# Two-bank score tiles, joint masked halves, and an eleventh weight pair in a hybrid attention and retention block

## The chip, the core and the metric

The kernel runs on one core of one Trainium2 chip. The metric is the device time of one execution in microseconds (us). A core has five engines that run at once, each through its own instruction stream: TensorE (PE in the profile; PEld is its weight load), VectorE (DVE), ScalarE (ACT), GpSimd (POOL) and SyncE (SP), which here only issues transfers. SBUF is the on-chip memory; PSUM is the memory that TensorE writes to, in eight banks, each a row of 512 float32 per partition.

## The reference

One decoder block on a sequence of 1024 with a model width of 1024. A single projection of the normalised input gives all branches; retention (A) and windowed attention (B) are gated, summed and projected, and a SwiGLU layer follows.

```python
h = rms_norm(x, ln1_g[l])
proj = h @ w_in[l] + b_in[l]
rq, rk, rv, rg, aq, ak, av, gate_a, gate_b = jnp.split(proj, SPLIT_IDX, axis=-1)
...
ay = sliding_window_sink_attention(aq, ak, av.reshape(B, S, ATTN_KV_HEADS, ATTN_HEAD_DIM), attn_sinks[l])
branch_b = ay.reshape(B, S, ATTN_Q) @ w_attn_out[l]
merged = jax.nn.sigmoid(gate_a) * branch_a + jax.nn.sigmoid(gate_b) * branch_b
x = x + merged @ w_out[l]
```

In the attention 16 query heads share 2 key/value heads. Queries stand in blocks of 128; each block sees its own and the previous block of keys, cut to a window of 128, and a sink value per head enters maximum and denominator:

```python
m = jnp.maximum(jnp.max(scores, axis=-1, keepdims=True), sink)
e = jnp.exp(scores - m)
probs = e / (jnp.sum(e, axis=-1, keepdims=True) + jnp.exp(sink - m))
out = jnp.einsum('bnhgqk,bnkhd->bnqhgd', probs.astype(v.dtype), vb)
```

## The kernel before, in words

Every product of matrices is made of float32 operands split in two, a high and a low part, and takes three matmuls of 128x512 (high x high, high x low, low x high). The split costs ScalarE a cast (the high part) and VectorE a subtraction (the low part) for each weight tile.

The program runs in stages: normalisation and the key and value projections of the attention, then the attention itself with part of the other projections as fill, then the v projection of the retention, the "w" stage, the retention core, the output projections and the SwiGLU layer.

**The attention.** A unit is one query block `b` (0 to 7) of one quad `g` (0 to 3) of four heads: 32 units. `u_scores` makes eight matmuls of 256 columns into two PSUM tiles "s" of a bank each (for `b = 0` the columns are half as many). Since a position of the window lies in exactly one of the two key blocks, ScalarE copies one block's scores to the tile `sc`, and VectorE overwrites the masked places with the other's (L537). A reduction takes the minimum with the sink, ScalarE takes four exponentials (L547, one per head, with their sums), VectorE the reciprocal, and the product normalises `sc`. Two iterations later `u_transpose` turns `sc` by TensorE and splits it into `ph` and `pl`; VectorE also makes masked halves `qh` and `ql` of them (L573), and `u_values` makes four matmuls: `ph`, `pl` with the values of one block, `qh`, `ql` with the difference of two blocks' values.

The result holds, for each head, two halves of sums that have still to be added. For quads 0 and 1, ScalarE copies it to `xy` and GpSimd issues a store to `xy_d`. For quads 2 and 3 the halves are added and split at once (L593 to L599), in place of the queries, and SP stores four parts of 1 MB to `ay_d`. In those quads half of the normalisation is done by ScalarE (L556).

The loop at L646 has 34 iterations. Iteration i takes unit i-2 through `u_transpose`, unit i through `u_scores`, then some steps of fill, then unit i-2 through `u_values`. A fill step is three matmuls 128x512 of the next item in the list `items`: the query projections of quads 1 to 3 (`QuadQ`: four times 24 matmuls, with a turning by ten operations of VectorE and four of ScalarE on each half) and twelve gate tiles (`Gate`: 2 x 24 matmuls). The steps are spread evenly, 244 in 34 iterations, and `fl.until` makes sure that a quad's queries are there before its units. TensorE and SP keep the program order in this loop. On VectorE and ScalarE a scheduler chooses the order, but for the splits of weights and of probabilities, which `tie` holds in program order. All engines then run their streams strictly in order.

**The v projection and the w stage.** The v projection is 28 products of a Strassen-Winograd scheme. VectorE first adds up its operands (`vadd`, L738) in `vacc`, which lies where the attention's buffers were. The w stage multiplies ten pairs of weight tiles (`cols`), each pair by seven products P1 to P7 of twelve matmuls instead of eight: pairs 0 to 7 are the retention's keys, queries and gates, the last two are four gate tiles. GpSimd makes the differences of weights (`gsub`, L676). `wseq` is the order of the products; splits are prepared three products ahead (`wprep_to`). P1, P6, P7 and P4 sum in one bank, and ScalarE copies it between them (`keep`, L968). At the end of this stage `split_ay` adds and splits the stored halves of quads 0 and 1 in eight pieces, one per product.

Of the kernel before, what the change touches and what calls it, by code (L numbers as in the profile page):

```python
# [35 lines left out]
def f32(t):  # L36
    return t.bitcast(F32)
# [3 lines left out]
def hybrid_block(ctx: ExitStack, tc: tile.TileContext, x, ln1_g, w_in, b_in, ret_norm_g, w_ret_out,  # L41
# [21 lines left out]
    ay_d = dram.tile([4, P, 4, S], F32, name="ay_d")  # L63
    xy_d = dram.tile([2, P, 4, S], F32, name="xy_d")
# [5 lines left out]

    def ps(tag, bufs, name):
        return psum.tile([P, 512], F32, tag=tag, bufs=bufs, name=name)

    def acc(name):
        return ps("acc", 3, name)

# [237 lines left out]
    with tc.tile_pool(name="gt", bufs=1, side="right") as gt, tc.tile_pool(name="w1", bufs=1) as w1:  # L314
# [7 lines left out]
        vodd = w1.tile([P, NB // 2, P], F32, tag="pl", bufs=1, name="vodd")  # L322
# [10 lines left out]
        lv = lo.rearrange("p k (z v e) -> p k z v e", z=2, v=2, e=32)  # L333
        def ak_evac(half, pt):
            c = slice(half * 512, half * 512 + 512)
            xb = r512(("ph", "qh")[half], 1, f"kxb{half}")
# [18 lines left out]
        def av_evac(half, pt):  # L355
            vt = r512("ql", 1, f"vt{half}")
# [159 lines left out]
        def u_scores(u):  # L516
# [9 lines left out]
            for jp in range(2):  # L526
                pt = ps("s", 2, f"s{g}{b}{jp}")
                for jj in range(2):
                    j = 2 * jp + jj
                    o = pt[:, jj * 256:jj * 256 + nk]  # L530
                    nc.tensor.matmul(o, Bt[:, jb + j, qc], kst[:, kv, 0, k0:k0 + nk], start=True, stop=False)
                    nc.tensor.matmul(o, Bt[:, jb + j, qc], kst[:, kv, 1, k0:k0 + nk], start=False, stop=True)
                jr = slice(2 * jp, 2 * jp + 2)
                if b > 0:
                    ptv = pt.rearrange("p (j z s) -> p j z s", j=2, z=2)
                    nc.scalar.copy(sc[:, jr, 0:P], ptv[:, :, 1])
                    nc.vector.copy_predicated(sc[:, jr, 0:P], mk.bitcast(U32).rearrange("p (o s) -> p o s", o=1)  # L537
                                              .to_broadcast([P, 2, P]), ptv[:, :, 0])
                    nc.vector.tensor_reduce(out=nm[:, jr], in_=sc[:, jr, 0:P + 1], op=ALU.min,  # L539
                                            axis=mybir.AxisListType.X)  # L540
                for jj in range(2):
                    j = 2 * jp + jj
                    if b == 0:
                        nc.vector.tensor_tensor_reduce(out=sc[:, j, 0:P], in0=pt[:, jj * 256:jj * 256 + P], in1=mk,
                                                       scale=1.0, scalar=nsink[:, 4 * g + j:4 * g + j + 1],
                                                       op0=ALU.add, op1=ALU.min, accum_out=nm[:, j:j + 1])
                    nc.scalar.activation(sc[:, j, 0:P + 1], sc[:, j, 0:P + 1], AF.Exp, scale=-1.0,  # L547
                                         bias=nm[:, j:j + 1], accum_out=den[:, j:j + 1])
            rd = tiny.tile([P, 4], F32, tag="rd", name=f"rd{g}{b}")
            nc.vector.reciprocal(rd, den)  # L550
            nd = 4 if g < 2 else 2
            nc.vector.tensor_tensor(out=sc[:, 0:nd, 0:P], in0=sc[:, 0:nd, 0:P],
                                    in1=rd[:, 0:nd].rearrange("p (j o) -> p j o", o=1).to_broadcast([P, nd, P]),
                                    op=ALU.mult)
            for j in range(nd, 4):
                nc.scalar.activation(sc[:, j, 0:P], sc[:, j, 0:P], AF.Copy, scale=rd[:, j:j + 1])  # L556

        def u_transpose(u):
            g, b, nk, Bt, jb, qc = geo(u)
            sc = scs.pop(u)  # L560
            pt = ps("t", 2, f"pT{g}{b}")
            for j in range(4):
                nc.tensor.transpose(pt[:, j * P:(j + 1) * P], sc[:, j, 0:P], ident)
            ph, pl = (w1.tile([P, 512], F32R, tag=t, bufs=1, name=f"{t}{g}{b}") for t in ("ph", "pl"))
            tie(acts, nc.scalar.copy(ph, pt))
            tie(vecs, nc.vector.tensor_tensor(out=pl, in0=pt, in1=f32(ph), op=ALU.subtract))
            phs[u] = [(vev[:, b // 2], ph, pl)]
            if b > 0:
                mk = amask[:, P:2 * P].rearrange("p (o s) -> p o s", o=1).to_broadcast([P, 4, P])
                part = []  # L570
                for t, src in (("qh", ph), ("ql", pl)):
                    o = w1.tile([P, 512], F32R, tag=t, bufs=1, name=f"{t}{g}{b}")
                    nc.vector.scalar_tensor_tensor(out=o.rearrange("p (j q) -> p j q", j=4), in0=mk,  # L573
                                                   scalar=float(b % 2 - 1), op0=ALU.add,
                                                   in1=f32(src).rearrange("p (j q) -> p j q", j=4), op1=ALU.mult)
                    part.append(o)
                phs[u].append((vdf[:, b - 1], *part))

        def u_values(u):
            g, b, nk, Bt, jb, qc = geo(u)  # L580
            pv = ps("pv", 1, f"pv{g}{b}")
            parts = phs.pop(u)
            for n, (vb, *hl) in enumerate(parts):
                for z, p in enumerate(hl):
                    nc.tensor.matmul(pv, vb[:, g // 2, :], p, start=(n + z == 0), stop=(n == len(parts) - 1 and z == 1))
            t = w1.tile([P, 512], F32, tag="xy", bufs=2, name=f"xy{g}{b}")
            if g < 2:
                nc.scalar.copy(t, pv)
                nc.gpsimd.dma_start(xy_d[g, :, :, qc], t.rearrange("p (j q) -> p j q", j=4))
                return  # L590
            pvv = pv.rearrange("p (i z q) -> p i z q", i=2, z=2)
            tm = t[:, 0:2 * P].rearrange("p (i q) -> p i q", i=2)
            nc.scalar.copy(tm[0:64], pvv[64:128, :, 0, :])  # L593
            nc.scalar.copy(tm[64:128], pvv[0:64, :, 1, :])
            nc.vector.tensor_tensor(out=tm[0:64], in0=pvv[0:64, :, 0, :], in1=tm[0:64], op=ALU.add)
            nc.vector.tensor_tensor(out=tm[64:128], in0=pvv[64:128, :, 1, :], in1=tm[64:128], op=ALU.add)
# [13 lines left out]
        order = list(range(6, 16)) + [0, 1]  # L610
        items = [QuadQ(0), QuadQ(1), Gate(order[0]), QuadQ(2), Gate(order[1]), QuadQ(3)] + [Gate(n) for n in order[2:]]
# [29 lines left out]
        run(filling(0))  # L641
        fl = Fill([filling(n) for n in range(1, len(items))])
        NU = 4 * NB
        fl.step(20)
        left = 32 * 8 - 8 - 4
        with in_order(nc.tensor.engine, nc.sync.engine):  # L646
            for i in range(NU + 2):
                if i % NB == 0 and 0 < i < NU:
                    fl.until((1, 3, 5)[i // NB - 1])
# [1395 lines left out]
```

## Time and profile before

| | |
|---|---|
| median of three runs | 1553.43 us (1551.37 to 1553.9) |
| profiled execution | 1554.05 us |
| its span in the trace | 1551.2 us |
| granted TensorE clock | 0.999 of full speed |
| attention with its fill | about 60 to 336 us of the span |
| v projection, then w stage | 336 to 413, 413 to 605 us |

The span runs from the first to the last instruction in the trace; the time of an execution has some 3 us more around it. A line of a timeline gives start, duration, engine, line of the kernel, operation, output and inputs; in brackets stands the idle time of the engine before it and what ended that. Matmuls overlap, so the distance of two starts, and not the duration shown, is what one costs. In the groups by shape a row ends with the busy time, the mean of one in ns, and the idle time before.

### The profile page before, as it was taken

How to read it: one execution, taken by the hardware profiler on the slowest of the kernel's cores; microseconds unless marked ns; L12 is line 12 of the kernel's file. 1: busy time of each engine (PE TensorE's matmuls, PEld its weight loads, DVE VectorE, ACT ScalarE, POOL GpSimd, SP SyncE). 2: the span in 40 equal slices, each digit the busy share in tenths (PEclk: the TensorE clock that was granted, in tenths of full speed). 3: DMA queues.
4: the chain of work that ended last, by engine and by line, in shares of the span. 5: the costliest groups of instructions: out<-in, count | busy, mean ns of one | idle time of the engine just before them, and what ended most of it. 6: DMA issues, size and time to landing. Idle time of an engine off the chain costs nothing.

```text
span 1551.2 us, 20530 instructions
## 1 busy us (share of the span) xinstructions
PE 1538.7 (99%) x7323; PEld 1284.9 (83%) x7323; DVE 1028.3 (66%) x1674; ACT 705.0 (45%) x1436; POOL 386.7 (25%) x336
## 2 busy tenths in 40 slices
PE   9999999999999999999999999999999999999998
PEld 8888888878888888888888888888888888888886
DVE  7578877788467675887457788444444444678656
ACT  6366677733233344544223465333333333444445
POOL 2001100000235440100111125655555555100001
PEclk9999999999999999999999999999999999999999
DMA  6665464331574456654556203333333333863233
GB/s 228 193 203 178 139 192 171 113 115 55 165 206 140 136 163 232 210 194 137 188 178 237 103 1 109 121 104 102 102 103 102 102 102 102 309 240 95 90 108 122
DMA packets 156402, 228.47 MB, mean 147 GB/s; under 512 B 10027, under 2 KB 82541, under 8 KB 156045
## 3 DMA queue, kind: packets, MB, share of 16 engines
q1 hardware_dynamic: 154972, 222.85, 44.3%
q0 software_dynamic: 1280, 4.20, 0.8%
q8 instruction: 57, 0.93, 0.2%
q14 instruction: 45, 0.36, 0.1%
q10 hardware_dynamic: 48, 0.13, 0.0%
HBM read 152.42 MB, written 69.99 MB: 143 GB/s over the span
## 4 chain that ended last, share of the span: by engine, by line
PE 86%; DVE 5%; ACT 4%; DMA 3%; issue 1%; SPq 0%; POOL 0%; POOLq 0%; DVEq 0%; ACTq 0%
PE fA L1669 15%; PE fB L1669 8%; PE dA L1971 7%; PE wA L963 6%; PE dxP L1971 6%; PE fC L1669 4%; PE wB L963 3%; PE va L807 3%; PE wo L1503 3%; PE woP L1503 2%; PE vP L807 2%; PE acc_ba L167 2%; PE acc_ba L169 2%; PE acc_ba L168 2%; PE acc_bb L167 2%; PE acc_bb L168 2%
## 5 line engine op out<-in xcount | busy, mean ns | idle before, releaser
L1971 PE MATMUL dA<-dwP,daP 128*128 128x512 f32 x528 | 120.6, 389 | 0.0
L1971 PEld LDWEIGHTS dA<-dwP,daP 128*128 128x128 f32 x528 | 99.1, 188 | 20.7 <-DVE dwP L143 0.2
L1971 PE MATMUL dxP<-dwP,daP 128*128 128x512 f32 x396 | 90.2, 389 | 0.0
L1971 PEld LDWEIGHTS dxP<-dwP,daP 128*128 128x128 f32 x396 | 74.3, 188 | 15.4
L167 PE MATMUL acc_g<-h,wh_g 128*128 128x512 f32 x192 | 75.3, 392 | 0.0
L168 PE MATMUL acc_g<-h,wh_g 128*128 128x512 f32 x192 | 74.9, 390 | 0.0
L169 PE MATMUL acc_g<-h,wl_g 128*128 128x512 f32 x192 | 74.8, 389 | 0.0
L547 ACT ACTIVATE sc<-sc,nm 128x129 f32<-128x129 f32 x128 | 50.2, 395 | 43.7 <-DVE nm L539 32.7
L1744 POOL TENSOR_TENSOR xf<-xf 128x512 f32<-128x512 f32 x40 | 62.3, 1557 | 30.3 <-issue 28.9
L523 POOL COPY sc<-nsink 128x4 f32<-128x4 f32 x32 | 9.9, 308 | 238.7 <-issue 73.0
L1675 POOL TENSOR_TENSOR xf<-xf 128x512 f32<-128x512 f32 x33 | 47.3, 1434 | 59.0 <-ACT xf L1677 26.9
L1876 POOL TENSOR_TENSOR rs_f<-tot,mhalf 128x1 f32<-128x1 f32 x8 | 4.8, 606 | 205.4 <-DVE tot L1873 205.4
L143 DVE TENSOR_TENSOR dwP<-wd,dwP 128x512 fp32r<-128x512 f32 x77 | 53.0, 688 | 4.3 <-ACT dwP L140 4.3
L140 ACT CAST dwP<-wd 128x512 fp32r<-128x512 f32 x77 | 47.4, 616 | 8.7 <-PE dA L1971 6.3
L140 ACT CAST daP<-daP 128x512 fp32r<-128x512 f32 x42 | 26.0, 621 | 55.4 <-PE dxP L1971 26.7
L167 PE MATMUL acc_bb<-ay,wh_bb 128*128 128x512 f32 x128 | 51.1, 400 | 0.0
L168 PE MATMUL acc_bb<-ay,wh_bb 128*128 128x512 f32 x128 | 50.1, 391 | 0.0
L169 PE MATMUL acc_bb<-ay,wl_bb 128*128 128x512 f32 x128 | 50.1, 391 | 0.0
L676 POOL TENSOR_TENSOR wr_wp<-wr_wp 128x512 f32<-128x512 f32 x10 | 15.7, 1570 | 137.9 <-DVE w0P L143 119.1
L167 PE MATMUL aq<-h,wh_aq 128*128 128x512 f32 x128 | 50.1, 391 | 0.0
L168 PE MATMUL aq<-h,wh_aq 128*128 128x512 f32 x128 | 50.0, 391 | 0.0
L167 PE MATMUL acc_ba<-yg,wh_ba 128*128 128x512 f32 x128 | 49.9, 390 | 0.0
(847 smaller groups left out, 4351.8 us busy)
## 6 DMA issues: line engine op xcount, KB each, us to landing
act_d<-xf SPq DMA_DIRECT2D x77, 256.0 KB, 2.1
daP<-act_d SPq DMA_DIRECT2D x21, 512.0 KB, 3.6
q<-q_d SPq DMA_DIRECT2D x32, 256.0 KB, 4.0
wr_daP<-act_d SPq DMA_DIRECT2D x14, 512.0 KB, 3.6
wr_g<-in_w_in SPq DMA_DIRECT2D x12, 512.0 KB, 5.9
tb_d<-tb SPq DMA_DIRECT2D x24, 256.0 KB, 4.9
wd<-in_w_ffn_down SPq DMA_DIRECT2D x6, 1024.0 KB, 13.5
wr_f<-in_w_ffn_gate SPq DMA_DIRECT2D x11, 512.0 KB, 4.0
```

Source lines behind the costliest of these rows:

```text
L140: nc.scalar.copy(hi, raw)
L143: return nc.vector.tensor_tensor(out=lo, in0=raw, in1=f32(hi), op=ALU.subtract)
L167: nc.tensor.matmul(pt, hi[:, k, :], xh, start=(k == 0), stop=False)
L168: nc.tensor.matmul(pt, hi[:, k, :], xl, start=False, stop=False)
L169: nc.tensor.matmul(pt, lo[:, k, :], xh, start=False, stop=(k == 7))
L547: nc.scalar.activation(sc[:, j, 0:P + 1], sc[:, j, 0:P + 1], AF.Exp, scale=-1.0, bias=nm[:, j:j + 1], accum_out=den[:, j:j + 1])
L807: nc.tensor.matmul(vbanks[pr][tt], x_[:, c], w[:, u, :], start=(fresh and k + z == 0), stop=(k == 3 and z == 2), skip_group_check=not fresh)
L963: nc.tensor.matmul(pt, o[:, w, k, :], v, start=(first and k + z == 0), stop=(k == 3 and z == 2), skip_group_check=not first)
L1503: nc.tensor.matmul(bank, v[:, q + u, k, c], w[y][:, k % 2, :], start=(first and z == 0), stop=(last and z == 2), skip_group_check=not tracked)
L1669: nc.tensor.matmul(pt, o[:, w, k, :], v, start=(first and n == 0), stop=(n == 11), skip_group_check=not first)
L1744: nc.gpsimd.tensor_tensor(out=o, in0=a, in1=b, op=op)
L1971: nc.tensor.matmul(banks[tt], a[:, u, c], w[:, v, :], start=(fresh and f + z == 0), stop=(f == NP - 1 and z == 2), skip_group_check=not fresh)
```

## The change

Four things change together.

1. The scores of a unit go into one PSUM tile of two banks, with one copy, one predicated copy and one reduction for all four heads. `ph` and `pl` become one tile `p`, and one operation of 128x1024 makes both masked halves `q`.
2. All quads are treated alike: ScalarE copies to `xy`, GpSimd stores to `xy_d` (32 stores instead of 16, of 256 KB), VectorE normalises all four heads. The sums and splits of quads 2 and 3 leave the attention; they become eight more pieces in the w stage, each with two loads, a sum, a cast, a low part and a store of 512 KB to `ay_d` by SP. The first eight pieces go to other products (from P6 of pair 8).
3. Gate tiles 0 and 1 leave the fill and become an eleventh pair. The last pair's order is P6, P5, P7, P2, P4, P3; before it was P6, P7, P5, P4, P3 with P2 made earlier.
4. The fill has ten gate tiles: seven steps an iteration for the first 16, then 96 steps over 18; 28 steps follow the loop, 24 before.

```diff
-            for jp in range(2):
-                pt = ps("s", 2, f"s{g}{b}{jp}")
...
-                    nc.scalar.copy(sc[:, jr, 0:P], ptv[:, :, 1])
-                    nc.vector.copy_predicated(sc[:, jr, 0:P], mk.bitcast(U32).rearrange("p (o s) -> p o s", o=1)
-                                              .to_broadcast([P, 2, P]), ptv[:, :, 0])
...
+            pt = spool[1].tile([P, 4, 2 * P], F32, tag="s4", name=f"s{g}{b}")
...
+                nc.scalar.copy(sc[:, :, 0:P], pt[:, :, P:2 * P])
+                nc.vector.copy_predicated(sc[:, :, 0:P], mk.bitcast(U32).rearrange("p (o s) -> p o s", o=1)
+                                          .to_broadcast([P, 4, P]), pt[:, :, 0:P])
+                nc.vector.tensor_reduce(out=nm, in_=sc[:, :, 0:P + 1], op=ALU.min, axis=mybir.AxisListType.X)
...
+                q = w1.tile([P, 2, 512], F32R, tag="q", bufs=1, name=f"q{g}{b}")
+                nc.vector.scalar_tensor_tensor(out=q.rearrange("p z (j q) -> p (z j) q", j=4), in0=mk,
+                                               scalar=float(b % 2 - 1), op0=ALU.add,
+                                               in1=f32(p).rearrange("p z (j q) -> p (z j) q", j=4), op1=ALU.mult)
...
-            if g < 2:
-                nc.scalar.copy(t, pv)
-                nc.gpsimd.dma_start(xy_d[g, :, :, qc], t.rearrange("p (j q) -> p j q", j=4))
-                return
...
-            v = Bt[:, jb:jb + 4, qc].rearrange("p (i z) q -> p i z q", z=2)
-            nc.scalar.copy(v[:, :, 0, :], tm)
-            nc.vector.tensor_tensor(out=v[:, :, 1, :], in0=tm, in1=f32(v[:, :, 0, :]), op=ALU.subtract)
+            nc.scalar.copy(t, pv)
+            nc.gpsimd.dma_start(xy_d[g, :, :, qc], t.rearrange("p (j q) -> p j q", j=4))
...
-        order = list(range(6, 16)) + [0, 1]
+        order = list(range(6, 16))
...
-        left = 32 * 8 - 8 - 4
+        early, late = 16 * 7, 96
...
-    cols += [C_GA + 256, C_GA + 512]
+    cols += [C_GA + 256, C_GA + 512, C_GA]
...
-        wseq += [(j, "P6"), (j, "P5"), (j, "P7"), (j + 1, "P1")] if nx else [(j, "P6"), (j, "P7"), (j, "P5")]
-        wseq += [(j, "P4"), (j, "P3")] + ([(j + 1, "P2")] if nx else [])
+        wseq += [(j, "P6"), (j, "P5"), (j, "P7"), (j + 1, "P1") if nx else (j, "P2"), (j, "P4"), (j, "P3")]
+        wseq += [(j + 1, "P2")] if j + 2 < NW else []
...
+    at8 = wseq.index((8, "P6"))
+    ayat = [(at8 + n, n) for n in range(8)] + list(zip((23, 26, 30, 37, 40, 44, 51, 54), range(8, 16)))
```

The scheduler's order on VectorE and ScalarE changes with it. Iteration 5 of the loop on VectorE before: `sc_1291` are the scores of unit 5, `ph_1283`, `pl_1284`, `qh_1287` and `ql_1289` the parts of unit 3, whose values end the same iteration.

```order
L566 TENSOR_TENSOR pl_1284<-pT_1278,ph_1283 128x512
L573 SCALAR_TENSOR_TENSOR qh_1287<-amask,ph_1283 128x512
L573 SCALAR_TENSOR_TENSOR ql_1289<-amask,pl_1284 128x512
L537 COPY_PREDICATED sc_1291<-amask,s_1295 128x2x128
L537 COPY_PREDICATED sc_1291<-amask,s_1305 128x2x128
L539 TENSOR_REDUCE nm_1293<-sc_1291 128x2 x2
L483 TENSOR_TENSOR st_1399<-q_1321,atab 128x512
L486 TENSOR_TENSOR q_1321<-q_1321,atab 128x512
L550 RECIPROCAL rd_1315<-den_1294 128x4
L552 TENSOR_TENSOR sc_1291<-sc_1291,rd_1315 128x4x128
```

The same iteration on VectorE after the change: `sc_1195` and `sc_1264` are units 4 and 5, `p_1259` and `q_1262` unit 3.

```order
L558 RECIPROCAL rd_1215<-den_1198 128x4
L559 TENSOR_TENSOR sc_1195<-sc_1195,rd_1215 128x4x128
L547 COPY_PREDICATED sc_1264<-amask,s_1268 128x4x128
L549 TENSOR_REDUCE nm_1266<-sc_1264 128x4
L558 RECIPROCAL rd_1284<-den_1267 128x4
L559 TENSOR_TENSOR sc_1264<-sc_1264,rd_1284 128x4x128
L452 TENSOR_TENSOR wl_aq_1235<-wr_aq_1053,wh_aq_1234 128x512
L570 TENSOR_TENSOR p_1259<-pT_1254,p_1259 128x512
L575 SCALAR_TENSOR_TENSOR q_1262<-amask,p_1259 128x1024
```

Unit 3's parts moved from ahead of unit 5's scores to behind all of that unit's operations. On ScalarE, before, in the same iteration:

```order
L588 COPY xy_1275<-pv_1270 128x512
L565 CAST ph_1283<-pT_1278 128x512
L536 COPY sc_1291<-s_1295 128x2x128
L536 COPY sc_1291<-s_1305 128x2x128
L474 ACTIVATE q_1321<-aq_1248,bcol 128x512
L547 ACTIVATE sc_1291,den_1294<-sc_1291,nm_1293 128x129 x4
```

And after:

```order
L589 COPY xy_1251<-pv_1246 128x512
L555 ACTIVATE sc_1195,den_1198<-sc_1195,nm_1197 128x129 x4
L546 COPY sc_1264<-s_1268 128x4x128
L555 ACTIVATE sc_1264,den_1267<-sc_1264,nm_1266 128x129 x4
L451 CAST wh_aq_1234<-wr_aq_1053 128x512
L569 CAST p_1259<-pT_1254 128x512
```

The cast of unit 3's probabilities moved behind the exponentials of units 4 and 5. In iteration 14 the same stands once more, with unit 14's scores ahead of unit 12's parts, but without an older unit's exponentials.

The end of the w stage on TensorE, before (`w9P` are the splits of the last pair's products, `wA` the bank that P1, P6, P7 and P4 share):

```order
L963 MATMUL wA_5566<-s_3677,w9P_5611 128x512 x12
L963 MATMUL wA_5566<-s_3677,w9P_5634 128x512 x12
L963 MATMUL wB_5696<-h_115,w9P_5656 128x512 x12
L963 MATMUL wA_5566<-h_116,w9P_5673 128x512 x12
L963 MATMUL wB_5696<-s4h,w9P_5693 128x512 x12
```

And after, where `w10P` is the eleventh pair:

```order
L957 MATMUL wA_5366<-s_3258,w10P_5381 128x512 x12
L957 MATMUL wB_5439<-h_118,w10P_5399 128x512 x12
L957 MATMUL wA_5366<-s_3258,w10P_5418 128x512 x12
L957 MATMUL wC_5479<-h_119,w10P_5435 128x512 x12
L957 MATMUL wA_5366<-h_119,w10P_5452 128x512 x12
L957 MATMUL wB_5439<-s4h,w10P_5476 128x512 x12
```

P6 and P7 (the first two in `wA`) now have P5 between them, and P2 (`wC`) stands between P7 and P4.

More of the change, by code (lines that the diff above doesn't have):

```diff
@@ new lines, in u_scores @@
+            pt = spool[1].tile([P, 4, 2 * P], F32, tag="s4", name=f"s{g}{b}")
+            for j in range(4):
+                for z in range(2):
+                    nc.tensor.matmul(pt[:, j, 0:nk], Bt[:, jb + j, qc], kst[:, kv, z, k0:k0 + nk], start=(z == 0),
+                                     stop=(z == 1))
+            if b > 0:
+                nc.scalar.copy(sc[:, :, 0:P], pt[:, :, P:2 * P])
+                nc.vector.copy_predicated(sc[:, :, 0:P], mk.bitcast(U32).rearrange("p (o s) -> p o s", o=1)
+                                          .to_broadcast([P, 4, P]), pt[:, :, 0:P])
+                nc.vector.tensor_reduce(out=nm, in_=sc[:, :, 0:P + 1], op=ALU.min, axis=mybir.AxisListType.X)
@@ new lines, in u_scores @@
+            for j in range(4):
+                if b == 0:
+                    nc.vector.tensor_tensor_reduce(out=sc[:, j, 0:P], in0=pt[:, j, 0:P], in1=mk, scale=1.0,
+                                                   scalar=nsink[:, 4 * g + j:4 * g + j + 1], op0=ALU.add, op1=ALU.min,
+                                                   accum_out=nm[:, j:j + 1])
+                nc.scalar.activation(sc[:, j, 0:P + 1], sc[:, j, 0:P + 1], AF.Exp, scale=-1.0, bias=nm[:, j:j + 1],
+                                     accum_out=den[:, j:j + 1])
@@ L549, in u_scores @@
             rd = tiny.tile([P, 4], F32, tag="rd", name=f"rd{g}{b}")
             nc.vector.reciprocal(rd, den)
[L551 to L556, printed above, removed]
+            nc.vector.tensor_tensor(out=sc[:, :, 0:P], in0=sc[:, :, 0:P],
+                                    in1=rd.rearrange("p (j o) -> p j o", o=1).to_broadcast([P, 4, P]), op=ALU.mult)
@@ L563, in u_transpose @@
                 nc.tensor.transpose(pt[:, j * P:(j + 1) * P], sc[:, j, 0:P], ident)
[L564 to L567, printed above, removed]
+            p = w1.tile([P, 2, 512], F32R, tag="p", bufs=1, name=f"p{g}{b}")
+            tie(acts, nc.scalar.copy(p[:, 0], pt))
+            tie(vecs, nc.vector.tensor_tensor(out=p[:, 1], in0=pt, in1=f32(p[:, 0]), op=ALU.subtract))
+            phs[u] = [(vev[:, b // 2], p)]
             if b > 0:
[L569 to L577, printed above, removed]
+                mk = amask[:, P:2 * P].rearrange("p (o s) -> p o s", o=1).to_broadcast([P, 8, P])
+                q = w1.tile([P, 2, 512], F32R, tag="q", bufs=1, name=f"q{g}{b}")
+                nc.vector.scalar_tensor_tensor(out=q.rearrange("p z (j q) -> p (z j) q", j=4), in0=mk,
+                                               scalar=float(b % 2 - 1), op0=ALU.add,
+                                               in1=f32(p).rearrange("p z (j q) -> p (z j) q", j=4), op1=ALU.mult)
+                phs[u].append((vdf[:, b - 1], q))
         def u_values(u):
@@ L897, in wprep_to @@
             wdone.add((j, pr))
-            if pr in ("P1", "P2") and {(j, "P1"), (j, "P2")} <= wdone:
+            both = {(j, "P1"), (j, "P2")} <= wdone
+            if pr == "P1" if j == NW - 1 else pr in ("P1", "P2") and both:
                 wtms[j] = wp.tile([P, 4, P], F32, tag="tt", bufs=1, name=f"wt2_{j}")
@@ L903, in wprep_to @@
                 gsub(b12, b22, b12)
+            if pr in ("P1", "P2") and both:
                 gsub(b21, b21, wtms[j])
```

130 lines of the change are left out of this document (69 added, 61 removed).

## The prediction

> **What bounds the kernel now.** I read the page first: totals, then the share of each engine in the chain that ended last.
>
> ```profile
> span 1551.2 us, 20530 instructions
> PE 1538.7 (99%) x7323; PEld 1284.9 (83%) x7323; DVE 1028.3 (66%) x1674; ACT 705.0 (45%) x1436; POOL 386.7 (25%) x336
> PE 86%; DVE 5%; ACT 4%; DMA 3%; issue 1%; SPq 0%; POOL 0%; POOLq 0%; DVEq 0%; ACTq 0%
> ```
>
> TensorE is busy for 1538.7 of 1551.2 us: 12.5 us are idle in all. So the change can win only by fewer matmuls or out of those 12.5 us, and it loses wherever TensorE is made to wait. Less work on VectorE and ScalarE is worth nothing by itself.
>
> The chain of waits prices a matmul. One product of the projection stage that follows the attention ("w" stage, twelve matmuls 128x512):
>
> ```profile
> 474.33 2.72 PE wC L963 x12
> ```
>
> That is 2.72 / 12 = 0.227 us each. The timeline of TensorE then shows one iteration of the attention loop without a stall (first transposes of the old unit's probabilities, then scores, fill, values, next transposes):
>
> ```profile
> 120.25 0.60 PE L563 MATMUL pT<-ident,sc 128*128 128x128 f32 x4
> ...
> 121.64 0.40 PE L167 MATMUL aq<-h,wh_aq 128*128 128x512 f32 x1
> ...
> 126.43 0.39 PE L585 MATMUL pv<-ph,vev 128*128 128x512 f32 x1
> ...
> 127.34 0.60 PE L563 MATMUL pT<-ident,sc 128*128 128x128 f32 x4
> ```
>
> Counted from an iteration's start, the scores end at 1.39, the values begin at 6.18, and the next iteration starts at 7.09 us. Values are four matmuls; the last two read the masked halves and begin at 6.63. Three matmuls 128x512 (one fill step) are 0.68 us.
>
> The same timeline has starts that lie further apart than 0.227 us; this is where TensorE waits. In the turning of the queries:
>
> ```profile
> 103.04 0.40 PE L585 MATMUL pv<-qh,vdf 128*128 128x512 f32 x1
> 103.91 0.50 PE L585 MATMUL pv<-ql,vdf 128*128 128x512 f32 x1 [0.47 <-DVE ql L573]
> ...
> 105.04 0.28 PE L532 MATMUL s<-kst,q 128*128 128x256 f32 x1
> 106.22 0.35 PE L531 MATMUL s<-kst,q 128*128 128x256 f32 x1 [0.90 <-DVE sc L537]
> ```
>
> At the end of the attention:
>
> ```profile
> 305.35 0.48 PE L585 MATMUL pv<-qh,vdf 128*128 128x512 f32 x1
> 305.93 0.50 PE L585 MATMUL pv<-ql,vdf 128*128 128x512 f32 x1
> ...
> 311.73 0.39 PE L585 MATMUL pv<-pl,vev 128*128 128x512 f32 x1
> 312.24 0.49 PE L585 MATMUL pv<-qh,vdf 128*128 128x512 f32 x1
> 312.84 0.50 PE L585 MATMUL pv<-ql,vdf 128*128 128x512 f32 x1
> ```
>
> And in the last pair of the w stage, where P6 and P7 follow each other in one bank and ScalarE copies between them:
>
> ```profile
> 592.26 1.75 PE L963 MATMUL wA<-s,w9P 128*128 128x512 f32 x7
> 594.69 1.66 PE L963 MATMUL wA<-s,w9P 128*128 128x512 f32 x6 [0.68 <-ACT u L968]
> ```
>
> **The change part by part.** *Two gate tiles to an eleventh pair.* Dense they are 2 x 2 x 24 = 96 matmuls, as a pair 7 x 12 = 84: twelve fewer, 12 x 0.227 = -2.72 us, nearly certain since TensorE has no other cover.
>
> *Last pair's order.* P6, P5, P7, P2, P4, P3 puts a product between P6 and P7. Seven matmuls from 592.26 should end at 593.85, the next starts at 594.69: -0.84 us. P5 covers that copy with 2.72 us.
>
> *Old waits of the attention.* The two starts at 103.91 and 106.22 are late by 0.87 - 0.23 = 0.64 and 1.18 - 0.12 = 1.06 (a 256-column matmul starts 0.12 after the last): -1.70, since the operations come in another order now. The three late ones at 305 to 313 are 0.35 + 0.28 + 0.37 = 1.00: -1.0, since nothing sums on chip there any more. Together these four parts give -6.26.
>
> *Wide operations.* The groups by shape price VectorE's and ScalarE's part of a unit:
>
> ```profile
> L566 DVE TENSOR_TENSOR pl<-pT,ph 128x512 fp32r<-128x512 f32 x29 | 20.0, 691 | 8.4 <-ACT ph L565 7.9
> L537 DVE COPY_PREDICATED sc<-amask,s 128x256 f32<-128x256 uint32 x50 | 19.4, 441 | 0.0
> L539 DVE TENSOR_REDUCE nm<-sc 128x2 f32<-128x258 f32 x50 | 18.6, 415 | 0.3
> L573 DVE SCALAR_TENSOR_TENSOR qh<-amask,ph 128x512 fp32r<-128x512 f32 x26 | 17.8, 683 | 0.0
> L459 DVE TENSOR_TENSOR wl_g<-wr_g,wh_g 128x1024 fp32r<-128x1024 f32 x11 | 13.4, 1220 | 1.0 <-ACT wh_g L458 1.0
> L552 DVE TENSOR_TENSOR sc<-sc,rd 128x512 f32<-128x512 f32 x13 | 9.0, 690 | 0.3
> L596 DVE TENSOR_TENSOR xy<-pv,xy 64x256 f32<-64x256 f32 x16 | 6.8, 428 | 0.2
> L588 ACT COPY xy<-pv 128x512 f32<-128x512 f32 x14 | 8.1, 579 | 6.7 <-PE pv L585 6.7
> ```
>
> No row shows a predicated copy or reduction of 512: between one 512-wide operation (0.69) and two of 256 (0.88 and 0.83) I take 0.70, since every 512-wide row here has 0.68 to 0.69. The joint masked half, 128x1024, lies between 1.22 (L459) and two of 0.683; I take 1.22, the row of its size. So a unit saves some 0.2 + 0.1 + 0.15 us of VectorE, and units of the last two quads lose L596 and its neighbours too. All of this lies beside TensorE: counted at nothing. The cover is the fill (6.18 - 1.39 us); where it fails, the next part counts.
>
> *The order inside the iterations.* Here the change costs. Four exponentials and the reciprocal behind them take, from the timeline of VectorE and ScalarE, 134.22 - 132.53 = 1.69 us:
>
> ```profile
> 132.53 0.41 ACT L547 ACTIVATE sc<-sc,nm 128x129 f32<-128x129 f32 x1 [0.59 <-DVE nm L539]
> 134.22 0.18 DVE L550 RECIPROCAL rd<-den 128x4 f32<-128x4 f32 x1 [0.26 <-ACT sc L547]
> ```
>
> Before, in iteration 5 VectorE made the halves of unit 3, which the same iteration's values need, ahead of unit 5's scores. Now it works through unit 5's scores first. From the iteration's start: ScalarE's copy xy of unit 2, queued ahead of unit 4's exponentials, ends at 0.6; exponentials 2.3; reciprocal and product (0.18 + 0.69) 3.2; predicated copy of unit 5 3.9; reduction 4.6; exponentials 6.3; reciprocal and product 7.1; a weight's low part 7.8; low part of p 8.5; masked halves 9.75. TensorE wants them at 6.63: +3.2 us (to the 0.1). Queued behind it on TensorE are the two last value matmuls and all of iteration 6. Iteration 14 has the same turn without the older unit's exponentials: scores end 1.39, copy 2.0, predicated copy 2.7, reduction 3.4, exponentials 5.1, reciprocal and product 6.0, weight 6.7, low part 7.4, halves 8.7: +2.1. Bounds of both together: 4.2, with the predicated copies and reductions at 0.44 and 0.42, to 6.2, with each wide operation at the price of two.
>
> In iterations 16 to 33 the fill is 96 steps in 18 iterations, 5 or 6 each instead of about 7: an iteration is 7.09 less one or two steps, 5.7 to 6.4 us. VectorE and ScalarE have a closed loop through it: low part 0.69, predicated copy 0.70, halves 1.22, reduction 0.70, exponentials 1.69, reciprocal and product 0.87: 5.9 us. That barely fits, and in iterations 21 and 22 the turning of the last quad's queries adds eight operations of 0.69 and a weight of 1.22. What lies between reduction and reciprocal is covered up to about 1.6; what is left is about 3.4 in two iterations, less a slack of 1.3 (halves are ready at 3.95 and the values of a 5.7 us iteration want them near 5.25): some 2.1 to 2.8, and 0.5 for iterations where exponentials stand behind an xy copy. I take +3.0, bounds 0 (the slack adds up over several iterations) and 5.
>
> *Start of the v projection.* VectorE's first sum there writes over the attention's buffers, so it must now wait for the last unit's store:
>
> ```profile
> 319.79 0.39 PE L585 MATMUL pv<-ql,vdf 128*128 128x512 f32 x1
> 322.84 2.36 DVE L738 TENSOR_TENSOR vacc<-h 128x1024 f32<-128x1024 f32 x2
> xy_d<-xy POOLq DMA_DIRECT2D x16, 256.0 KB, 4.7
> ```
>
> Before, the sum starts 3.05 us after the last value matmul. Now matmul, copy and landing are 0.23 + 0.58 + 4.7 = 5.5, so it comes at least 2.5 us later; four more fill steps stand before the products (28 instead of 24), 4 x 0.68 = 2.7 us. I take +0.5 for what GpSimd needs to issue, bounds 0 to 2.
>
> *Eight more pieces in the w stage.* Each adds a sum and a low part on VectorE, a cast, two loads and a store on SP. The windows of the stage:
>
> ```profile
> 474.00:540.00 66.00, 66.00 (x293) 54.66 (x292) 42.65 (x50) 24.57 (x43) 30.21 (x22) 1.00 0.49 149
> ```
>
> VectorE (third column after the length) has 23.35 us free in 66. A sum with both inputs in SBUF takes 0.69, or 1.78 where GpSimd works beside it:
>
> ```profile
> 441.49 0.69 DVE L935 TENSOR_TENSOR r<-r,rtabkT 128x512 f32<-128x512 f32 x1 [2.16 <-DMA xw<-r]
> 450.59 1.78 DVE L935 TENSOR_TENSOR r<-r,rtabkT 128x512 f32<-128x512 f32 x1
> ...
> 450.08 1.74 POOL L676 TENSOR_TENSOR wr_wp<-wr_wp 128x512 f32<-128x512 f32 x1
> ```
>
> Eight pieces are 8 x (0.69 + 0.69) = 11 to 8 x (1.78 + 0.69) = 20 us over 31 products, 84 us: it fits on average, as weights are split three products ahead. I take +0.6, bounds 0 to 8. SP holds its later transfers behind a piece's store; the weights behind it are loaded two pairs ahead, some 14 x 2.72 us of cover. [...]
>
> The sum: -6.26 + 3.2 + 2.1 + 3.0 + 0.5 + 0.6 = +3.1. The profiled execution took 1554.05 us (its span 1551.2 and 2.85 around it), 0.62 above the median: 1554.05 + 3.1 - 0.62, so 1556.6 us against 1553.43.
>
> **The rivals.** *The lag is absorbed (B).* The new turns cost no more than the old one did, 1.70, because its rows are the only such turn the trace shows; the late loop fits and the pieces hide. Then -6.26 + 1.70, so 1548.9. For it: 1.70 is measured, and the late loop's 5.9 lies within its iterations' 5.7 to 6.4. Against: iterations 5 and 14 are fixed orders, and their chain is longer than the fill. It decides where the halves are ready before 6.63.
>
> *Only the two turned iterations (C).* The late loop keeps up: -6.26 + 5.3 + 0.5, so about 1553.0: no change. For it: buffers for three units of probabilities let the loop spread.
>
> *VectorE fails in the w stage (D).* Each piece holds a weight's split by the 1.09 us between the two rows of L935: 8.7 in place of 0.6, so about 1564.7. It decides where three products, 8.2 us, no longer cover VectorE's queue. For it: 20 of 84 us on an engine with about a third free. Against: TensorE has no idle time in that window.
>
> **How the numbers follow.** The forecast case (A) has 0.48, B 0.24, C 0.18, D 0.10. About 0.2% or 3.1 us is what a measurement here can tell from no change: bounds 1550.3 and 1556.5. A lies on the upper one; its own range is 1553.5 to 1561, of which I count 0.28 slower and 0.20 within. B gives 0.22 faster and 0.02 within, C 0.16 within and 0.02 faster, D 0.10 slower. So faster 0.24, same 0.38, slower 0.38. The range takes in A, C and most of B, from 1548 to 1562; D and B's tail are left out.
>
> **What would show it.** Right: in iterations 5 and 14 the masked value matmuls start 3 and 2 us late, released by VectorE's halves; further such waits in iterations 21 to 23; no gap between P6 and P7 of the last pair; TensorE busy for about 2.7 us less. Wrong: value matmuls that never wait for the halves (B), waits only in 5 and 14 (C), or TensorE waiting for weight splits at the pieces (D).

## The result, and the profile after

The changed kernel takes 1560.36 us (median of six runs, 1559.52 to 1562.59), against 1553.45 for the kernel before (six runs). The ratio is 1.005, 95% interval 1.0037 to 1.0063: about 7 us slower. The forecast was 1556.6: the sign is right, and of the 6.9 us it had 3.1.

The page of the changed kernel, the same three lines as before:

```profile
span 1558.6 us, 20393 instructions
PE 1539.6 (99%) x7311; PEld 1283.1 (82%) x7311; DVE 1030.0 (66%) x1566; ACT 690.5 (44%) x1360; POOL 404.2 (26%) x356
PE 88%; DVE 4%; DMA 3%; ACT 2%; issue 1%; SPq 1%; POOL 0%; POOLq 0%; DVEq 0%; ACTq 0%
```

TensorE has twelve matmuls less, and yet 19.0 us without work instead of 12.5 (span less busy time). VectorE lost 108 instructions and is as busy as before.

Where the time went is read from the chains of waits, at the start of the v projection and at the first transposes behind the w stage. Before:

```profile
336.52 11.18 PE va L807 x48
605.88 0.88 PE kTT L1074 x8
```

And after:

```profile
110.52 6.92 DMA wr_aq<-in_w_in
325.13 11.17 PE va L800 x48
...
607.22 2.72 PE wA L957 x12
609.94 2.72 PE wB L957 x12
612.66 0.87 PE kTT L1097 x8
```

The v projection starts 11.4 us earlier, but 96 matmuls of fill (96 x 0.227 = 21.8 us) left the attention: it lost 10.4 us. From there to the transposes it is 287.5 in place of 269.4, 18.2 more for 84 matmuls that cost 19.0: the stage wins 0.9, the last pair's wait, and the last products follow each other every 2.72 us. So all of the loss up to there lies in the attention. And the chain has a link that the attention's chain of before did not have: a weight load (`wr_aq`) of 6.92 us.

The timeline of TensorE at the values of four iterations, with the idle time in brackets:

```profile
118.62 0.50 PE L586 MATMUL pv<-p,vev 128*128 128x512 f32 x1 [1.63 <-ACT p L569]
119.46 0.49 PE L586 MATMUL pv<-p,vev 128*128 128x512 f32 x1 [0.34 <-DVE p L570]
120.72 0.72 PE L586 MATMUL pv<-q,vdf 128*128 128x512 f32 x2 [0.77 <-DVE q L575]
...
184.63 0.50 PE L586 MATMUL pv<-p,vev 128*128 128x512 f32 x1 [0.19 <-ACT p L569]
185.79 0.49 PE L586 MATMUL pv<-p,vev 128*128 128x512 f32 x1 [0.65 <-DVE p L570]
187.04 1.22 PE L586 MATMUL pv<-q,vdf 128*128 128x512 f32 x2 [0.76 <-DVE q L575]
...
239.36 0.73 PE L586 MATMUL pv<-q,vdf 128*128 128x512 f32 x2 [2.26 <-DVE q L575]
...
276.42 0.73 PE L586 MATMUL pv<-q,vdf 128*128 128x512 f32 x2 [1.04 <-DVE q L575]
```

The first three rows are iteration 5, the next three iteration 14, the last two iterations 22 and 28; 23 and 29 wait 0.2 each. Counted by the distance of starts, iteration 5 loses 3.6 us, iteration 14 2.3 us of waits, the late ones together 4.9. Behind iteration 14 the clock falls too. These are windows behind the two waits (a row has the stretch, its length, the busy time of each engine, then the granted clock, which is the third number from the end):

```profile
122.00:123.00 1.00, 1.00 (x10) 0.96 (x9) 0.41 (x1) 0.68 (x3) 0.53 (x1) 1.00 0.00 0
...
186.00:188.00 2.00, 1.24 (x3) 0.72 (x3) 0.99 (x1) 0.00 (x0) 0.00 (x0) 0.76 0.35 131
188.00:189.00 1.00, 1.00 (x6) 0.94 (x5) 0.00 (x0) 0.58 (x1) 0.00 (x0) 0.50 0.00 0
```

Behind iteration 5 the clock is whole, behind iteration 14 it is halved for 3.4 us (187.0 to 190.4): the last two value matmuls take 0.6 us more there, the transposes and scores behind them 1.1.

The wide operations, by shape, cost about what the prediction took (0.70, 0.70, 1.22):

```profile
L547 DVE COPY_PREDICATED sc<-amask,s 128x512 f32<-128x512 uint32 x28 | 20.4, 728 | 1.1 <-ACT sc L546 1.1
L549 DVE TENSOR_REDUCE nm<-sc 128x4 f32<-128x516 f32 x28 | 19.2, 686 | 1.0
L575 DVE SCALAR_TENSOR_TENSOR q<-amask,p 128x1024 fp32r<-128x1024 f32 x28 | 34.1, 1219 | 0.4
```

### The profile page after: what moved, and what is told of

Its sections match the earlier page's. It is cut to its first block, busy times and chain, and to the rows that moved or that the text cites. A ratio compares the mean times of both kernels' runs of the same rounds, so it can differ in the third digit from the quotient of the medians.

```text
span 1558.6 us, 20393 instructions
## 1 busy us (share of the span) xinstructions
PE 1539.6 (99%) x7311; PEld 1283.1 (82%) x7311; DVE 1030.0 (66%) x1566; ACT 690.5 (44%) x1360; POOL 404.2 (26%) x356
## 4 chain that ended last, share of the span: by engine, by line
PE 88%; DVE 4%; DMA 3%; ACT 2%; issue 1%; SPq 1%; POOL 0%; POOLq 0%; DVEq 0%; ACTq 0%
PE fA L1692 15%; PE fB L1692 8%; PE dA L1994 7%; PE wA L957 7%; PE dxP L1994 6%; PE fC L1692 4%; PE wB L957 3%; PE va L800 3%; PE wo L1526 3%; PE woP L1526 2%; PE vP L800 2%; PE acc_ba L178 2%; PE acc_ba L180 2%; PE acc_ba L179 2%; PE acc_bb L179 2%; PE acc_bb L180 2%
## 5 line engine op out<-in xcount | busy, mean ns | idle before, releaser
L178 PE MATMUL acc_g<-h,wh_g 128*128 128x512 f32 x160 | 62.7, 392 | 0.0
L179 PE MATMUL acc_g<-h,wh_g 128*128 128x512 f32 x160 | 62.5, 391 | 0.0
L180 PE MATMUL acc_g<-h,wl_g 128*128 128x512 f32 x160 | 62.3, 389 | 0.0
L669 POOL TENSOR_TENSOR wr_f<-wr_f 128x512 f32<-128x512 f32 x20 | 30.7, 1533 | 76.0 <-DVE t_18P L154 8.6
```

The costliest lines, as they stand in the source:

```text
L178: nc.tensor.matmul(pt, hi[:, k, :], xh, start=(k == 0), stop=False)
L179: nc.tensor.matmul(pt, hi[:, k, :], xl, start=False, stop=False)
L180: nc.tensor.matmul(pt, lo[:, k, :], xh, start=False, stop=(k == 7))
```

## The experiments

Each is named by its number; times are medians, ratios (with their 95% intervals) are against the kernel before on the same chip. Its median was 1552.65 us beside runs 1 to 4, 1553.25 beside 5 to 8 and 1553.70 beside 9 to 12, so between runs of different groups the ratios count, and a difference of 1 to 2 us is hardly told from none.

**1. The order held.** Of the changed kernel, the copy of the scores, the predicated copy and the masked halves go into the chains that keep program order.

```diff
-                nc.scalar.copy(sc[:, :, 0:P], pt[:, :, P:2 * P])
+                tie(acts, nc.scalar.copy(sc[:, :, 0:P], pt[:, :, P:2 * P]))
```

(and so for `copy_predicated` and the `scalar_tensor_tensor` of `q`, with `vecs`)

> The changed kernel with only an order added: the copy of a unit's scores (ScalarE), the predicated copy and the masked halves (VectorE) are held in program order behind the parts of the unit two iterations older. Theory (the two turned iterations cost 3.5 and 3.2 us, the late loop some 4.9): the waits in iterations 5 and 14 go, those in 22 and 28 stay: 1560.4 - 6.7 = 1553.7, between 1552.5 and 1556. Rival (VectorE and ScalarE have too little time in an iteration, the order only decides where it shows): the waits come out elsewhere, 1558 to 1561.

1558.51 us, 1.0043 (1.0029 to 1.0056): of 6.7 us only 1.9 came back by the medians, 1.1 by the ratios. Iteration 14's waits went. Iteration 5's stayed (3.5 us of waits in place of 3.4), for another reason. ScalarE's timeline there:

```profile
117.39 0.62 ACT L451 CAST wh_aq<-wr_aq 128x512 fp32r<-128x512 f32 x1 [4.29 <-DMA wr_aq<-in_w_in]
117.92 0.58 ACT L569 CAST p<-pT 128x512 fp32r<-128x512 f32 x1
```

ScalarE has nothing to do for 4.29 us: the cast of the third quad's weights waits for their load, and the cast of unit 3's probabilities is held behind it by the chain that was in the kernel already. In the changed kernel the same cast waited 0.41 us only, since the turned order had kept ScalarE busy with unit 5's exponentials up to 117.06. So two causes lay side by side; by these rows the order alone would have cost at most 0.4 us less (an estimate: no run has the turned order with an early load). The windows show why the loss in this iteration is even larger here:

```profile
118.00:120.00 2.00, 1.01 (x2) 0.37 (x2) 1.92 (x3) 1.57 (x4) 0.00 (x0) 0.99 0.08 31
120.00:122.00 2.00, 1.35 (x4) 1.05 (x5) 1.90 (x3) 0.09 (x1) 0.00 (x0) 0.50 0.35 131
...
127.00:128.00 1.00, 1.00 (x6) 0.79 (x5) 0.49 (x1) 1.00 (x2) 0.00 (x0) 1.00 0.00 0
```

From 120.0 on TensorE runs at half its clock for 6.8 us. The first matmuls 128x512 behind the wait stand 0.43 us apart instead of 0.23; together the half clock costs some 3 us here.

**2. An even fill.**

```diff
-        early, late = 16 * 7, 96
+        left = 26 * 8
...
-                n, i0, m = (early, 0, 16) if i < 16 else (late, 16, NU - 14)
-                fl.step((i - i0 + 1) * n // m - (i - i0) * n // m)
+                fl.step((i + 1) * left // (NU + 2) - i * left // (NU + 2))
```

> The changed kernel with 208 fill steps spread evenly over the 34 iterations (6 or 7 each) in place of 7 and then 5 or 6. The scheduler's order still has two turned iterations, now 6 and 16. Theory: the turned iterations still cost 3 to 3.5 us each, the late waits of 4.9 us fall below 1.5: about 1556.5. Rival (the turns are harmless, the late loop alone is the loss): no wait in 6 and 16, about 1550. Rival (too little time in every iteration): waits only spread, 1559 to 1561.

1558.73 us, 1.0037 (1.0024 to 1.0049): between the theory and the third case. The late waits fell to some 2.8 us, not below 1.5, but iteration 4 waits 1.3 and iterations 13 and 14 some 1.9. Of the two turned iterations 6 costs 4.7 us with its clock (the transposes behind the wait take 1.06 us there in place of 0.60), 16 only 0.5. An even fill gives to the late iterations what the early ones need.

**3. The pair alone.** On the kernel before: `cols` with the eleventh pair, the new last order, ten gate tiles in the fill (208 steps evenly), the eight old pieces on the last pairs.

> The kernel before with the eleventh pair and the last pair's new order alone; its fill has ten gate tiles, 208 steps evenly. Scores stay in two tiles, quads 2 and 3 are still summed on chip. Theory: the pair gives -2.7 and its order -0.9; the shorter iterations (6.1 steps, 6.4 us) nearly fill VectorE in the last two quads, whose units need about 6.2 us of it: waits of 0 to 3 us there: 1550 to 1553. Rival (the on-chip sums don't fit any more into the shorter iterations, so they had to be moved): 1555 or more. No wait at P6 to P7 of the last pair under either.

1556.98 us, 1.0029 (1.0018 to 1.0041): the part that was to win loses 4.3 us by itself, so the rival's number came true, but only in part at its place. The last two quads wait some 3.6 us, never over 0.7 at once. The largest loss is in iteration 3, where the second quad's queries are turned (VectorE, TensorE):

```profile
98.70 0.68 DVE L566 TENSOR_TENSOR pl<-pT,ph 128x512 fp32r<-128x512 f32 x1
99.31 0.68 DVE L483 TENSOR_TENSOR st<-q,atab 128x512 f32<-128x512 f32 x1
...
102.31 0.69 DVE L573 SCALAR_TENSOR_TENSOR qh<-amask,ph 128x512 fp32r<-128x512 f32 x1
```

```profile
103.05 0.50 PE L585 MATMUL pv<-qh,vdf 128*128 128x512 f32 x1 [2.67 <-DVE qh L573]
```

Five turning operations stand between `pl` and the half that TensorE wants; the second half costs another 1.0, and the clock drops after this wait too: it is 0.69 on average from 104 to 108 and 0.88 from 108 to 112, and the fill's matmuls from 106.35 to 108.48 start 0.43 us apart. With 7.2 steps an iteration the same place cost 1.7 us, with 6.1 it costs 3.8 and the slow matmuls behind it.

**4. The wide operations alone.** On the kernel before: one two-bank score tile, `p` and `q`, all four heads normalised by VectorE; nothing else.

> The kernel before with the wide operations alone (scores in one two-bank tile, joint masked halves, all four heads normalised by VectorE); sums on chip, ten pairs and twelve gate tiles in the fill as before. No iteration is turned in its order. Theory (wide operations cost nothing by themselves): within 1.5 us of before, 1552 to 1554, predicated copy and reduction 0.65 to 0.75 us, joint halves near 1.25. Rival (one tile for all scores makes copy and exponentials wait for the last matmul and lengthens each unit's chain): waits in many iterations, 1556 or more.

1552.74 us, 1.0 (0.9991 to 1.0009): no change, as the theory said. The prediction's zero holds as a sum, but not because everything stays hidden. In the profiled execution (1554.07 us) two new waits stand in iterations 9 and 10, and from the second on the granted clock is 0.50 for 3.4 us:

```profile
148.19 0.73 PE L586 MATMUL pv<-q,vdf 128*128 128x512 f32 x2 [0.80 <-DVE q L575]
150.12 1.85 PE L543 MATMUL s<-kst,q 128*128 128x256 f32 x8 [0.76 <-DVE sc L547]
```

With the clock they cost 3.7 us. Against that, the late starts at 305 to 313 of the kernel before are gone, and the waits of iterations 3 and 4 are 0.7 us shorter. The sums on chip are still there in this run, so the prediction's reason for the late starts (the sums) is not what ended them.

**5. The weight load first.** Of the changed kernel, one thing in `filling`:

```diff
-            send_turned()
             at = 23 if it.size == 2 else 4 if n + 1 < len(items) and items[n + 1].size == 2 else 0
+            if at:
+                send_turned()
```

Where `at` is 0, the next item's `prep`, which issues a load, now comes ahead of the stores of the turned queries.

> The changed kernel with one thing moved: where a gate tile begins, SP issues the next weight load before the turned queries' stores and loads, not behind them (the second slab of quads 2 and 3 waited there). No tie is added; the scheduler's order then has unit 3's and unit 12's parts ahead of the newer unit's exponentials. Theory (the late slab is the cause of both long waits: the weight's cast waits for it, the cast of the probabilities is held behind that cast, and the scheduler turned the iteration round because of it): waits in iterations 5 and 14 go, the late ones stay: 1553 to 1555. Rival (the order is the scheduler's own choice, the load only happens to end at the same time): waits of 3 us stay in 5 or 14, 1557 to 1561.

1554.65 us, 1.0009 (1.0 to 1.0018): one moved step brings 5.7 us back by the medians, 6.4 by the ratios. SP's timeline shows the load in the changed kernel:

```profile
107.14 3.33 SPq L519 DMA_DIRECT2D q<-q_d  x4
110.52 0.43 SPq L442 DMA_DIRECT2D wr_aq<-in_w_in  x1
```

and in this run:

```profile
93.49 0.42 SPq L442 DMA_DIRECT2D wr_aq<-in_w_in  x1
...
107.12 3.33 SPq L519 DMA_DIRECT2D q<-q_d  x4
```

The load goes out 17 us earlier. Without any tie the scheduler then puts unit 3's and unit 12's parts ahead of the newer units' exponentials again (unit 3's still behind unit 5's predicated copy and reduction). Iteration 14 does not wait, iteration 5 loses 0.7 us. That the scheduler turned them because it reckoned with a late slab fits all this but was only argued: the runs show that moving the load moves the order.

**6. Both: order held, load first.**

> Both: the order held as in the first experiment, and the weight load issued first. Theory: the wait of iteration 5 that the held order had left (and the half clock behind it, some 2 us) goes: 1558.5 - 6 = 1552.5, within 1.5 us of the kernel with the load alone. Rival (too little time on VectorE and ScalarE): another iteration takes the wait over, 1556 or more.

1553.53 us, 1.0 (0.9992 to 1.0009): better than the held order alone by 5.0 us in the medians, 6.7 by the ratios. Iteration 5 has no wait. Of what is left, some 2.6 us lie in iterations 7, 11 and 12 and 4.3 in the late ones, half of these in iteration 22:

```profile
231.20 0.68 DVE L506 TENSOR_TENSOR q<-q,st 128x512 fp32r<-128x512 f32 x1
231.80 1.22 DVE L575 SCALAR_TENSOR_TENSOR q<-amask,p 128x1024 fp32r<-128x1024 f32 x1
```

```profile
233.07 0.74 PE L586 MATMUL pv<-q,vdf 128*128 128x512 f32 x2 [1.77 <-DVE q L575]
```

The turning of the last quad's queries (eight operations of VectorE on each half, not ten; L506 is the last) stands ahead of the halves, in an iteration of five steps.

**7. Even fill and load first.**

> The changed kernel with an even fill and the weight load issued first. Theory: no turned iteration (they cost 3.6 and more in the even fill) and late waits of 2 to 3 in place of 4.9: 1551 to 1553.5. Rival: the even fill only moves waits from the late iterations to the early ones, no better than the load alone, 1554 or more.

1556.14 us, 1.0016 (1.0007 to 1.0025): the theory failed; the rival's number came true, but for a reason neither side named. The attention's waits are about those of run 5, but the w stage of the profiled execution waits 4.8 us (1.2 in the changed kernel), though its code is the same. Its executions spread from 1553.50 to 1559.99 us, and the profiled one took 1557.69. VectorE and TensorE there:

```profile
525.28 1.83 DVE L929 TENSOR_TENSOR r<-r,rtabkT 128x512 f32<-128x512 f32 x1 [4.61 <-DMA xw<-r]
527.03 0.68 DVE L1020 TENSOR_TENSOR ayp<-ays,ayp 128x512 fp32r<-128x512 f32 x1
527.63 1.16 DVE L154 TENSOR_TENSOR w6P<-wp,w6P 128x512 fp32r<-128x512 f32 x1
```

```profile
528.85 2.56 PE L957 MATMUL wA<-h,w6P 128*128 128x512 f32 x10 [1.43 <-DVE w6P L154]
```

VectorE, in program order there, waits for swapped halves that come through SP's queue; a piece's low part and the weight's split stand behind.

**8. No pair.** The changed kernel with ten pairs, the old last order, and twelve gate tiles in 244 even steps.

> The changed kernel without its eleventh pair: ten pairs with the old last order, twelve gate tiles in the fill, 244 steps evenly; wide operations, all results stored and the eight pieces in the w stage stay. Its order has the turned iterations 5 and 14. Theory (those come from the late slab, not from the shorter fill): 3 us waits in both stay, late waits go since an iteration has 7.2 steps again: 1553.4 - 2.7 (old waits) + 6.7 = 1557.5. Rival (the waits come from iterations made shorter by the missing gate tiles): none in 5 and 14, 1551 to 1553.

1558.65 us, 1.003 (1.0018 to 1.0042): iterations 5 and 14 wait with a full fill as well (3.2 and 2.2 us), and the late waits are gone, as the theory said. So the late waits come from shorter iterations and the first two do not; that those come from where the load stands, run 5 shows. It also shows the cover that the prediction named for the v projection. With 24 steps of rest its first products wait for VectorE's splits (this once, and 1.23 four us later):

```profile
346.84 3.03 PE L799 MATMUL va<-vP,h 128*128 128x512 f32 x12 [1.08 <-DVE vP L154]
```

With 28, in the changed kernel, they don't.

**9. The exponentials held.** Run 6, and `tie(acts, ...)` around the four exponentials and the copy `xy` too.

> The repaired kernel (order held, weight load first) with ScalarE's exponentials and its copy xy also held in program order, so that a unit's exponentials never stand behind the copy of the older unit's result, which waits for TensorE. Theory (those copies explain the waits of iterations 27 and 31, some 1.6 us, not the one of iteration 22, where VectorE turns the queries): 1553.5 - 1.5 = 1552. Rival (the held exponentials delay the weights' casts on ScalarE): 1554 or more, with waits for weights.

1564.61 us, 1.0069 (1.0056 to 1.0082): the theory failed, by far. Some ten iterations wait, and the granted clock is 0.50 for 3.4 us behind one of them. In that one VectorE stands before a turning operation whose tile is still being stored, with the reciprocal of a unit behind it:

```profile
226.69 0.69 DVE L497 TENSOR_TENSOR st<-q,atab 128x512 f32<-128x512 f32 x1 [2.92 <-DMA q_d<-st]
227.30 0.17 DVE L558 RECIPROCAL rd<-den 128x4 f32<-128x4 f32 x1
```

Holding one engine's order moved another's; why the scheduler put that operation there stays open.

**10. Sums on chip.** Run 6, with quads 2 and 3 added and split in the attention as before.

> The repaired kernel with quads 2 and 3 summed and split in the attention as before, no late pieces in the w stage; wide operations, eleventh pair, the uneven fill stay. Theory (a unit of these quads then takes VectorE about 5.9 us of 5.7 to 6.4, and the sums stand in its queue between the halves): waits of 3 to 8 us in iterations 18 to 33, 1555 to 1560. Rival (the sums were hidden and moving them gained nothing): late waits no larger than 5 us, no waits from pieces in the w stage, 1552 to 1554.

1558.07 us, 1.0028 (1.0017 to 1.004): 4.5 us worse than run 6. The largest wait is again in the turning iteration, now with the sums in it (L506 ends the turning, L601 is a sum's low part; VectorE, then TensorE):

```profile
232.96 0.68 DVE L506 TENSOR_TENSOR q<-q,st 128x512 fp32r<-128x512 f32 x1
233.56 0.42 DVE L601 TENSOR_TENSOR q<-xy,q 128x256 fp32r<-128x256 f32 x1
234.01 0.69 DVE L570 TENSOR_TENSOR p<-pT,p 128x512 fp32r<-128x512 f32 x1
```

```profile
234.75 0.50 PE L586 MATMUL pv<-p,vev 128*128 128x512 f32 x1 [1.82 <-DVE p L570]
```

So with the shorter fill, moving the sums away is worth 4 to 5 us.

**11. No late pieces.** Run 7 without the eight late pieces. The halves of quads 2 and 3 are not added or split, they go into the output projection as they were stored.

> The kernel with the even fill and the weight load first, whose w stage waited 4.8 us for weight splits, without the eight late pieces: the two halves of quads 2 and 3 go unadded and unsplit into the output projection, straight from where they were stored. Theory (the pieces' loads and stores on SP hold up the swapped halves that VectorE waits for, and the sums themselves stand in its queue): waits in the w stage fall to 1.5 us or less: 1553. Rival (these waits belong to the splits of eleven pairs): unchanged, 1555.5 to 1557.

1563.02 us, 1.0058 (1.0045 to 1.0071): its time says nothing on the pieces, since the output projection now waits for these loads. Its windows still bear on the question. First run 7, then this one, from 474 us to the end of the stage (in run 7 the first two of the eight sums lie ahead of that, at 463.5 and 470.4):

```profile
474.00:540.00 66.00, 64.19 (x282) 52.54 (x281) 45.09 (x54) 25.00 (x44) 28.29 (x18) 1.00 0.74 214
540.00:605.00 65.00, 64.02 (x282) 52.35 (x281) 42.91 (x58) 32.59 (x57) 20.73 (x14) 1.00 0.51 166
```

```profile
474.00:540.00 66.00, 66.00 (x293) 54.66 (x292) 41.69 (x49) 24.64 (x44) 29.42 (x21) 1.00 0.46 137
540.00:605.00 65.00, 65.00 (x289) 53.81 (x288) 39.14 (x53) 32.76 (x56) 17.18 (x12) 1.00 0.42 135
```

TensorE's 2.8 us of waits there vanish with the pieces. Ahead of the first sum it waits for weight splits in both runs, 1.2 us in run 7 and 2.4 here, so the stage does not fall to the 1.5 us of the theory.

**12. The last quad's queries earlier.** Run 6, and:

```diff
-        items = [QuadQ(0), QuadQ(1)] + [Gate(n) for n in order[0:2]] + [QuadQ(2)] + [Gate(n) for n in order[2:4]]
-        items += [QuadQ(3)] + [Gate(n) for n in order[4:]]
+        items = [QuadQ(0), QuadQ(1)] + [Gate(n) for n in order[0:2]] + [QuadQ(2), QuadQ(3)] + [Gate(n) for n in order[2:]]
...
-                    fl.until((1, 4, 7)[i // NB - 1])
+                    fl.until((1, 4, 5)[i // NB - 1])
```

> The repaired kernel (order held, weight load first) with the last quad's query projection right behind the third's, so that its turning falls into iterations with seven fill steps, and the gate tiles after it. Theory (the wait of iteration 22, 1.9 us, and its neighbours come from ten turning operations in a short iteration): these go and nothing comes back, 1551 to 1552. Rival (any iteration that turns queries waits; early units with the xy copy are as full): the wait moves to the iteration of the turning, 1553 to 1556.

1551.41 us, 0.9987 (0.9978 to 0.9996): 2 us better than the kernel before. The page, and the longest wait left at the values on TensorE:

```profile
span 1548.8 us, 20393 instructions
PE 1536.1 (99%) x7311; PEld 1282.1 (83%) x7311; DVE 1027.0 (66%) x1566; ACT 690.6 (45%) x1360; POOL 403.6 (26%) x356
```

```profile
196.29 0.73 PE L586 MATMUL pv<-q,vdf 128*128 128x512 f32 x2 [0.90 <-DVE q L575]
```

The waits of iterations 22, 28 and 32 (4.0 us in run 6) are nearly gone. The rival is right in part: the turning now ends in iteration 16, which has five steps, and this one loses 1.6. TensorE is idle for 12.7 us, about as in the kernel before (12.5), with twelve matmuls less: the change brings its 2.7 us only once its waits are no longer than those of before.

## Why the prediction was right, and where not

*The pair and the last order: right.* -2.72 and -0.84 were forecast; the stretch from the v projection to the transposes shows both within 0.1 us. One sign did not come: TensorE's busy time is 0.9 us longer and not 2.7 shorter, as a late value matmul that stands alone counts as busy for 0.50 us in place of 0.23 in the stream, and the half clock lengthens others (the two masked value matmuls are shown with 1.22 us in iteration 14 and 0.72 in iteration 5). In run 12 it is 2.6 shorter.

*The old waits: the number right.* None of the five late starts of before is there. That the last three go because nothing sums on chip any more does not hold: in run 4 they go with the sums in place.

*Wide operations at nothing: right as a sum,* by run 4's time. Their rows are as reckoned, but in run 4 they moved waits about.

*Iteration 5, +3.2: the size right, 3.6; the cause only half.* (The steps listed add up to 9.75 - 6.63 = 3.1.) The chain of operations was the one reckoned, and the halves came 10.0 us behind the iteration's start in place of 9.75. But a second cause of about the same length lay under it, a weight load behind the turned queries' transfers on SP. The step that failed is "Now it works through unit 5's scores first", taken as the whole. Run 1 undid the order and won nothing there; run 5 moved the load, the order changed with it, and 0.7 us were left; run 6 did both, and nothing was left. That the size came out is partly luck, since the load would have given it too.

*Iteration 14, +2.1: the waits right, 2.3.* The half clock behind it, 1.7 us, was in no term. No run shows what sets it off. The half clock lasted 3.4 us in the changed kernel and 6.8 in run 1, and iteration 5 kept its clock (1.00) in the changed kernel and lost it (0.50) in run 1 after nearly the same wait. Nor does the busy time ahead tell the cases apart: TensorE was busy for some 1.3 of the 3.4 us before the fall in run 1 and for 1.8 in iteration 14, but for only 1.0 of the 3.4 us before the masked value matmuls of iteration 5 in the changed kernel (117.3 to 120.7), and there the clock stayed.

*The late loop, +3.0: undersized, 4.9.* Iterations 22 and 23 lose 3.0, as the turning was reckoned, but 28 and 29 another 1.8, where 0.5 had been set for the exponentials behind an xy copy. Run 8 shows that these waits end with a full fill, run 12 that moving the turning takes away most of them.

*The v projection, +0.5: none.* VectorE's first sum does wait for the last store (5.4 us idle up to 310.19), but the four steps more cover it, and run 8 shows the wait without them. No row or run gives the 0.5 that was taken for GpSimd's issue; the row of one issue of such a store has 0.72 us (POOL L590, at 112.03).

*The pieces, +0.6: at most 0.1 in this kernel.* The price of 1.78 for a sum beside GpSimd does not hold for every row: before, L935 took 1.78 us at 450.59 (GpSimd at work from 450.08) and 1.52 at 479.75 (from 479.42), but 0.69 at 441.49, where the operation of GpSimd from 441.50 on took 1.82. After the change the eight late sums (L1011) took 0.68 to 0.70, none with an operation of GpSimd beside it. But the term is not stable: 2.8 us in run 7's profiled execution by the same code, as run 11 shows. It stays far below the 8 of the bound.

Over the forecast of 3.1 come iteration 14's clock (1.7), the late loop (1.9), the first two waits (0.6) and small waits in other iterations (0.6, what is left of the attention's 10.4), less 1.1 for the last two terms: 6.8 up to the transposes. The spans differ by 7.4; the last 0.6 lies behind the w stage, where the same code took 945.9 us in place of 945.3. Of the rivals, B failed since the new turns cost more than the old 1.70; C since the late loop did not keep up, and its two iterations alone came to 7.6 with the clock; D did not come in this kernel.

## What to carry to other kernels

Where TensorE is full, taking work out of its fill can cost more than the work (run 3: twelve matmuls less, 4.3 us more): ask for each stage what the fill was covering, and price the iteration in which another job (here the turning of queries) meets it. A wait found in an order may have a second cause of equal length below it: a load's place in SP's queue belongs in the reckoning, and undoing the first cause alone may win nothing. When a scheduler sets an engine's order, each edit can move waits in stages it does not touch (run 7, run 9), so parts measured alone do not add up.

## What was not expected of the hardware

In run 1 a wait of some 3 us on TensorE cost more than itself: the granted clock behind it was 0.50 for 6.8 us, though two matmuls had run within the wait, and matmuls stood 0.43 us apart instead of 0.23. In the changed kernel a wait of 3.6 us at the same place left the clock at 1.00.
